# Turning the first head group's probabilities by transposing DMAs instead of TensorE in a two-layer encoder trunk

## The chip, the cores and the metric

The kernel runs on one core of a Trainium2 chip. The metric is the device time of one execution in microseconds: 1993.09 us before the change (median of three runs, 1992.59 to 1994.17). The engines of the core are named as in the profile: PE (matmul, with its weight loads as PEld), DVE (vector), ACT (scalar), POOL (gpsimd) and SP, whose queue issues nearly all DMAs.

## What is computed

Two layers of an encoder on 256 tokens of width 2048. Each layer has eight attention heads of 128 in two groups of four (each group shares one key and one value head), with a window of 128 tokens, a spatial gating part, an output projection and a gated feed-forward part with a short convolution.

```python
h = rms_norm(x, norm1_g[l])
q, k, v, gu, gv = jnp.split(h @ w_in[l], splits, axis=-1)
q = apply_rope(rms_norm(q...)); k = apply_rope(rms_norm(k...))
attn = banded_window_attention(q, k, v, sink[l])      # softmax with a sink in the denominator
sgu = chunked_spatial_gating(gelu(gu), gelu(gv), ...)  # layer norm of gv, 128x128 product, times gu
mixed = concat([rms_norm(attn), rms_norm(sgu)])
x = x + mixed @ w_o[l]
x = x + conv_gated_ffn(rms_norm(x, norm2_g[l]), w_up[l], conv_w[l], conv_b[l], w_down[l])
```

All is float32. The kernel makes a float32 product from three products of a rounded part (hi) and its rest (lo).

## The kernel before

**Weights.** They come in blocks of 1 MB. SP issues the load of a block into one of three `raw` buffers (L120), ACT rounds it in two halves to `hi` (L128, 128x1024 each, four buffers), and DVE subtracts to get `lo` (L112, four buffers). A block of the input or output projection is used by 24 matmuls of 512 columns (L168); a gate unit (L194 on) has 32 matmuls with hi (L209) and 32 half as wide with lo (L214). The blocks of a layer's input projection come as chunks of four: queries of the first group, keys and values, queries of the second group, two chunks of gv, then four gate units (gu), then w_o, w_up and w_down.

**Attention.** `attend` (L466) is a generator, made once per head group: `first` (g = 0) and `second` (g = 1). Its steps are called between weight blocks, by lists that are written out by hand (`between`, and the arguments of `gated`). The steps: take q from PSUM, rotate it and compute its norm (a power on POOL, `qr`, then L477); copy the halves of the 32-bit words apart (L422) and send them through transposing DMAs of 128x4x128 words (L429); copy them together (L435) and split them in hi and lo (L302 on ACT, L303 on DVE); then per pair of heads the products with the keys (L308 to L310, three matmuls each) into `tp`, a PSUM pool of **two** buffers, the masked scaling and maximum on DVE (L498, which empties `tp`), the exponential on ACT (L520), the sum and its inverse, and the scaling by it (L528). Then per pair of heads the probabilities are turned by PE (L536, four 128x128 transposes per 128 keys), split in parts (L302, L303, from PSUM), multiplied with the values (L308 to L310, 512 columns) and copied out of PSUM by ACT (L545).

**Gating.** gv's chunks are taken from PSUM (L723), go through a gelu on ACT (L724), statistics on DVE (L725, L729) and a power on POOL (L733, `lnr`). `normal` (L768 to L770) normalises the four `vn` tiles with tables that `gating_tables` loads (two loads at L408, six at L413); `spatial` (L751) multiplies them with the 128x128 tables, four units of 128x512 outputs.

**Order.** A scheduler orders the instructions of each engine by priority. `urgent()` raises the priority of what stands in it, weight loads and their parts among them. Every engine works through its own list in that order, and an instruction that waits holds up all behind it on its engine. `take` (L188) lets a step start only behind the matmul issued last. Tiles in SBUF come from the pool `slots` (43 of them), rows from `rowp`.

Of the kernel before, what the change touches and what calls it, by code (L numbers as in the profile page):

```python
# [8 lines left out]
F32 = mybir.dt.float32  # L9
F32R = mybir.dt.float32r  # L10
# [5 lines left out]
P = 128  # L16
# [26 lines left out]
def encoder(ctx: ExitStack, tc: tile.TileContext, xT, x, w_in, w_gu, w_o, w_up, w_down, wsT, pcol, prow, rope, out):  # L43
# [1 line left out]
    pool = lambda name, bufs, **kw: ctx.enter_context(tc.tile_pool(name=name, bufs=bufs, **kw))  # L45
    const = pool("const", 1)
    lay = pool("lay", 2)
    slots = pool("slots", 43)
    rowp = pool("rowp", 4)
    evp = pool("evp", 4)  # L50
    rawp = pool("rawp", 3)
# [8 lines left out]
        return slots.tile(shape, dt, tag="sl", name="sl")  # L60

    def row(tag):
        return rowp.tile([P, W], F32, tag=tag, name=tag)

    def ev():
        return evp.tile([P, 2, SEQ], F32, tag="ev", name="ev")
# [10 lines left out]
    def tp(shape):  # L77
        return tpp.tile(shape, F32, tag="tp", name="tp")
# [339 lines left out]
    def apart(srcs):  # L418
        halves = []
        for src in srcs:  # L420
            h = sl([P, 2, 2 * P], U16)
            nc.scalar.copy(h, src.bitcast(U16).rearrange("p (n b) -> p b n", b=2))  # L422
            halves.append(h)
        return halves

    def sent(halves):
        tall = sl([P, 4, SEQ], U16)
        for m in range(2):
            nc.sync.dma_start_transpose(tall[:, :, m * P : (m + 1) * P], halves[m].rearrange("p b n -> p (b n)"))  # L429
        return tall  # L430

    def together(tall):
# [33 lines left out]
    def attend(g, ps, r, kT, v, tab, qk, nsink, acc, pc, outs):  # L466
        ms = st([P, 2, 4], "qms")
        rot = []
        for m in range(2):
            q = row("q")  # L470
            with urgent():
                nc.scalar.activation(q, ps[:, m, :], AF.Copy, scale=r[:, m : m + 1])
            head_squares(q, 4, ms[:, m, :])
            rot.append(rotate(q, m, 4, tab))
        qr = inv_rms(ms.rearrange("p a b -> p (a b)"), HD, "q", 8)
        qs = st([P, 8], "qs")
        nc.vector.tensor_scalar_mul(qs, qr, HD**-0.5)  # L477
        rows = [rot[m].rearrange("p h d -> p (h d)") for m in range(2)]
        halves = [apart([rows[m][:, h : h + 2 * HD] for m in range(2)]) for h in (0, 2 * HD)]
        yield  # L480
        talls = [sent(h) for h in halves]
        yield
        qT = []
        for tall in talls:
            pq = parts(together(tall), [P, 2, SEQ])
            qT += [[v[:, i, :] for v in pq] for i in range(2)]
        yield
        scores = []
        for pr in range(2):
            nmx = st([P, 2, 2], "nmx")  # L490
            for i in range(2):
                h = 2 * pr + i
                t = tp([P, 2, SEQ])
                s = sl([P, 2, SEQ])
                for m in range(2):
                    matmul3(t[:, m, :], [v[:, m * P : (m + 1) * P] for v in qT[h]], [v[:, g, :] for v in kT])
                for m in range(2):
                    nc.vector.tensor_tensor_reduce(  # L498
                        out=s[:, m, :],
                        in0=t[:, m, :],  # L500
                        in1=mask[:, m, :],
                        scale=qs[:, 4 * m + h : 4 * m + h + 1],
                        scalar=LOWEST,
                        op0=ALU.add,
                        op1=ALU.max,
                        accum_out=nmx[:, i, m : m + 1],
                    )
                scores.append(s)
            h0 = 4 * g + 2 * pr
            sink = qk[:, R_SINK + h0 : R_SINK + h0 + 2].unsqueeze(2).to_broadcast([P, 2, 2])  # L510
            nsk = nsink[:, h0 : h0 + 2].unsqueeze(2).to_broadcast([P, 2, 2])
            nm = st([P, 2, 2], "nm")
            nc.vector.scalar_tensor_tensor(out=nm, in0=nmx, scalar=-1.0, in1=nsk, op0=ALU.mult, op1=ALU.min)
            es = st([P, 2, 2], "es")
            nc.vector.tensor_tensor(out=es, in0=nm, in1=sink, op=ALU.add)
            rs = st([P, 2, 2], "rs")
            for i in range(2):
                s = scores[2 * pr + i]
                for m in range(2):
                    nc.scalar.activation(s[:, m, :], s[:, m, :], AF.Exp, bias=nm[:, i, m : m + 1], accum_out=rs[:, i, m : m + 1])  # L520
            nc.scalar.activation(es, es, AF.Exp)
            nc.vector.tensor_tensor(out=rs, in0=rs, in1=es, op=ALU.add)
            rec = st([P, 2, 2], "rec")
            nc.vector.reciprocal(rec, rs)
            for i in range(2):
                s = scores[2 * pr + i]
                for m in range(2):
                    nc.vector.tensor_scalar_mul(s[:, m, :], s[:, m, :], rec[:, i, m : m + 1])  # L528
            yield
        for pr in range(2):  # L530
            pT = []
            for b in range(2):
                t = tp([P, 2, SEQ])
                for i in range(2):
                    for m in range(2):
                        nc.tensor.transpose(  # L536
                            t[:, i, m * P : (m + 1) * P], scores[2 * pr + i][:, m, b * P : (b + 1) * P], ident
                        )
                pT.append(parts(t.rearrange("p a b -> p (a b)"), [P, W]))
# [83 lines left out]
    for l in range(DEPTH):  # L623
# [48 lines left out]
        for m in range(2):  # L672
# [2 lines left out]
                out=a, in0=a, in1=rk[:, 2 * m : 2 * m + 2].unsqueeze(2).to_broadcast([P, 2, HD]), op=ALU.mult  # L675
            )
            krot.append(a)
        vs = [parts(kv[m][:, 2 * HD :], [P, 2 * HD]) for m in range(2)]
        kT = []

        khalves = apart([a.rearrange("p h d -> p (h d)") for a in krot])
# [24 lines left out]
        r1b = as_rows(r1)  # L706
        second = group_steps(1, ps)
        second()
        ws, lrows = gating_tables(l)


        vn = []
        stats = st([P, 2, 2, 6], "bns")
        for i in range(2):
            if l:
                between = [[[first], [first], [], [first]], [[first, second], [first], [second, first], [second]]]
            else:
                between = [[[first], [first], [first], [second]], [[second], [], [first], [first]]]
            ps = chunk(3 + i, between[i])
            for m in range(2):  # L720
                t = row("vn")
                with urgent():
                    nc.scalar.activation(t, ps[:, m, :], AF.Copy, scale=r1[:, m : m + 1])  # L723
# [218 lines left out]
```

## Time and profile before

| | |
|---|---|
| the three runs | 1992.59, 1993.09, 1994.17 us |
| the profiled execution | 1992.69 us, of which its span is 1990.9 us |
| PE clock granted | 1.000 |
| DMA | 391.15 MB, 196 GB/s on average |
| weight load of 1 MB, issue to landing | 4.9 to 5.2 us |

The profile is of one execution of the kernel. Its page gives busy times by engine, the span in 40 slices, DMA queues, the chain of work that ended last and the costliest groups of instructions; further views list waits, groups by line and shape, and instructions in order of time. A row of the view in order of time holds the start, the time to the end of the row's last instruction, engine and line, and after x how many instructions were merged in it. The stage that the change touches lies between 70 and 180 us (layer 0) and between 1063 and 1180 us (layer 1).

### The profile page before, as it was taken

The numbers are of one execution on the slowest core, as the hardware profiler recorded it, in microseconds if no ns is written. First come the engines' busy times: TensorE is split into PE (matmuls) and PEld (weight loads), VectorE is DVE, ScalarE is ACT, GpSimd is POOL, SyncE is SP. The second block draws the span as 40 slices with busy tenths as digits, with TensorE's granted clock in tenths as the row PEclk, the third lists the DMA queues.
The fourth block names the chain that finished last, engine by engine and source line by source line (L and its number), as shares of the span: only waits on it lengthen the run. The fifth ranks groups of instructions, "written<-read, shape, count | busy, mean of one in ns | idle before, by whom it ended". The sixth has DMA issues, their size and how long they took to land.

```text
span 1990.9 us, 26332 instructions
## 1 busy us (share of the span) xinstructions
PE 1985.5 (100%) x10292; PEld 1704.8 (86%) x10292; DVE 1367.6 (69%) x1930; ACT 1134.5 (57%) x1514; POOL 23.3 (1%) x25
## 2 busy tenths in 40 slices
PE   9999999999999999999999999999999999999999
PEld 8888888888888888888888888888888888888887
DVE  6778677777754577775566786777777445777753
ACT  6786585556543455556667675855555344555542
POOL 0100000000000000000000000000000000000000
PEclk9999999999999999999999999999999999999999
DMA  9754674455555544556767536745545554455563
GB/s 341 243 161 149 219 222 169 170 208 207 198 191 192 188 170 174 212 207 204 219 205 237 161 142 226 198 169 206 207 180 211 191 192 167 171 208 203 201 212 127
DMA packets 95580, 391.15 MB, mean 196 GB/s; under 512 B 43744, under 2 KB 45024, under 8 KB 50912
## 3 DMA queue, kind: packets, MB, share of 16 engines
q1 hardware_dynamic: 94736, 388.74, 56.6%
q8 instruction: 80, 1.31, 0.3%
q10 hardware_dynamic: 720, 0.73, 0.1%
q14 instruction: 44, 0.36, 0.1%
HBM read 378.43 MB, written 2.10 MB: 191 GB/s over the span
## 4 chain that ended last, share of the span: by engine, by line
PE 97%; ACT 1%; DVE 1%; DMA 1%; issue 0%; SPq 0%; POOL 0%; DVEq 0%; ACTq 0%
PE mm L168 42%; PE mm L234 31%; PE mm L240 16%; PE mm L209 2%; PE mm L275 1%; PE tp L168 1%; PE mm L214 1%; PE mm L270 1%; PE tp L308 0%; PE tp L751 0%; PE tp L310 0%; DVE lo L112 0%; PE tp L309 0%; DMA raw<-in_w_up 0%; ACT hi L128 0%
## 5 line engine op out<-in xcount | busy, mean ns | idle before, releaser
L112 DVE TENSOR_TENSOR lo<-raw,hi 128x1024 fp32r<-128x1024 f32 (+1 forms) x708 | 839.4, 1215 | 417.4 <-ACT hi L128 277.1
L128 ACT ACTIVATE hi<-raw 128x1024 fp32r<-128x1024 f32 (+1 forms) x708 | 730.3, 1050 | 606.8 <-PE mm L168 330.9
L168 PE MATMUL mm<-hi,sl 128*128 128x512 f32 x2480 | 667.6, 390 | 0.1
L234 PE MATMUL mm<-sl,hi 128*128 128x512 f32 x2688 | 617.8, 389 | 0.2 <-ACT hi L128 0.2
L234 PEld LDWEIGHTS mm<-sl,hi 128*128 128x128 f32 x2688 | 501.9, 188 | 103.5 <-ACT hi L128 1.1
L168 PEld LDWEIGHTS mm<-hi,sl 128*128 128x128 f32 x2480 | 464.5, 188 | 97.2 <-DVE sl L289 0.9
L168 PE MATMUL mm<-lo,sl 128*128 128x512 f32 x1240 | 382.6, 390 | 0.0
L240 PEld LDWEIGHTS mm<-sl,lo 128*128 128x128 f32 x2688 | 328.1, 192 | 3.3
L240 PE MATMUL mm<-sl,lo 128*128 128x256 f32 x2688 | 329.1, 283 | 0.0
L168 PEld LDWEIGHTS mm<-lo,sl 128*128 128x128 f32 x1240 | 232.5, 188 | 47.9
L838 DVE SCALAR_TENSOR_TENSOR sc<-ev,pc,sc 128x255 f32<-128x255 f32 x176 | 80.6, 481 | 94.0 <-ACT sc L837 94.0
L281 ACT COPY ev<-mm 128x512 f32<-128x512 f32 x96 | 55.4, 577 | 122.5 <-PE mm L240 114.8
L837 ACT ACTIVATE sc<-ev,pc 128x256 f32<-128x256 f32 x176 | 99.1, 589 | 0.0
L841 DVE SCALAR_TENSOR_TENSOR sc<-ev,pc,sc 128x255 f32<-128x255 f32 x176 | 80.6, 481 | 2.9
L296 ACT ACTIVATE sl<-sl 128x256 fp32r<-128x256 f32 x88 | 31.8, 409 | 72.8 <-DVE sl L857 72.8
L283 DVE TENSOR_TENSOR ev<-mm,ev 128x512 f32<-128x512 f32 x96 | 65.6, 683 | 0.0
L209 PE MATMUL mm<-sl,hi 128*128 128x512 f32 x256 | 61.6, 391 | 0.0
L833 DVE TENSOR_TENSOR ev<-ev,rb 128x512 f32<-128x512 f32 x88 | 60.1, 682 | 0.1
L209 PEld LDWEIGHTS mm<-sl,hi 128*128 128x128 f32 x256 | 47.3, 188 | 9.2
L289 DVE SCALAR_TENSOR_TENSOR sl<-sl,pc 128x256 fp32r<-128x256 f32 x96 | 42.6, 479 | 17.7 <-ACT sl L288 17.6
L297 DVE TENSOR_TENSOR sl<-sl 128x256 fp32r<-128x256 f32 x88 | 33.5, 422 | 19.4 <-ACT sl L296 19.4
L288 ACT ACTIVATE sl<-sl,pc 128x256 fp32r<-128x256 f32 x96 | 43.2, 497 | 1.1 <-DMA sl<-in_xT 0.9
(124 smaller groups left out, 813.2 us busy)
## 6 DMA issues: line engine op xcount, KB each, us to landing
raw<-in_w_up SPq DMA_DIRECT2D x172, 1024.0 KB, 5.2
raw<-in_w_down SPq DMA_DIRECT2D x88, 1024.0 KB, 4.9
raw<-in_w_in SPq DMA_DIRECT2D x38, 1024.0 KB, 5.1
raw<-in_w_o SPq DMA_DIRECT2D x32, 1024.0 KB, 4.9
raw<-in_w_gu SPq DMA_DIRECT2D x16, 1024.0 KB, 4.9
raw<-in_w_up SPq DMA_DIRECT2D x8, 512.0 KB, 4.5
sl<-in_prow SPq DMA_DIRECT2D x12, 256.0 KB, 7.3
raw<-in_w_in SPq DMA_DIRECT2D x8, 256.0 KB, 5.2
```

What stands on the lines that cost most here:

```text
L112: nc.vector.tensor_tensor(out=lo, in0=part, in1=hi.bitcast(F32), op=ALU.subtract)
L128: nc.scalar.activation(hi[:, cs], part, AF.Copy)
L168: nc.tensor.matmul(ps[m], acts[kk][:, part % 2, m * P : (m + 1) * P], w, start=first and kk == 0 and part == 0, stop=last and kk == KB - 1 ...
L209: nc.tensor.matmul(ps[:, i, :], tile_of(his, k, i), x1, start=k == 0, stop=False)
L234: nc.tensor.matmul(pss[n][:, i, :], hs[k // KB][:, c : c + P], x1, start=k == 0, stop=False)
L240: nc.tensor.matmul(pss[n][:, i, :SEQ], los[k // KB][:, c : c + P], acts[k][:, 0, :], start=False, stop=k == len(acts) - 1)
L281: nc.scalar.copy(rest, ps[:, :, SEQ:])
L283: nc.vector.tensor_tensor(out=s, in0=ps[:, :, :SEQ], in1=rest, op=ALU.add)
L833: nc.vector.tensor_tensor(out=s, in0=s, in1=r2b2[0], op=ALU.mult)
L837: nc.scalar.activation(t[:, i, :], s[:, i, :], AF.Identity, bias=col(3), scale=col(1))
L838: nc.vector.scalar_tensor_tensor(out=t[:, i, 1:], in0=s[:, i, : SEQ - 1], scalar=col(0), in1=t[:, i, 1:], op0=ALU.mult, op1=ALU.add)
L841: nc.vector.scalar_tensor_tensor(out=t[:, i, : SEQ - 1], in0=s[:, i, 1:], scalar=col(2), in1=t[:, i, : SEQ - 1], op0=ALU.mult, op1=ALU.add)
```

## The change

For the first group the sixteen PE transposes of a layer go. Behind the scaling of a pair's scores, ACT copies each head's tile apart into two halves of 16-bit words (L538), SP sends each through one DMA transpose of 128x8x128 words (L547), and DVE joins the halves again in the layout that PE wrote before (L559, two copies for each 128 keys of a pair); the parts hi and lo then come from SBUF. The second group keeps the transposes on PE (now L565). The first group has two more steps, and the hand-written lists are shared out anew. The transposes of keys and queries become urgent (L430). The gating tables are asked for behind the two gv chunks instead of ahead of them. Values' hi and lo share a slot, q's four copies of 128x512 become two of 128x1024 (L483), `slots` grows from 43 to 46 and the rows for q shrink from four to two.

```diff
-    slots = pool("slots", 43)
+    slots = pool("slots", 46)
...
-        return rowp.tile([P, W], F32, tag=tag, name=tag)
+        return rowp.tile([P, W], F32, tag=tag, name=tag, bufs=2 if tag == "q" else 4)
...
     def sent(halves):
         tall = sl([P, 4, SEQ], U16)
-        for m in range(2):
-            nc.sync.dma_start_transpose(tall[:, :, m * P : (m + 1) * P], halves[m].rearrange("p b n -> p (b n)"))
+        with urgent():
+            for m in range(2):
+                nc.sync.dma_start_transpose(tall[:, :, m * P : (m + 1) * P], halves[m].rearrange("p b n -> p (b n)"))
...
-        halves = [apart([rows[m][:, h : h + 2 * HD] for m in range(2)]) for h in (0, 2 * HD)]
+        both = []
+        for m in range(2):
+            t = sl([P, 2, 2, 2 * HD], U16)
+            words = rot[m].rearrange("p h d -> p (h d)").bitcast(U16)
+            nc.scalar.copy(t, words.rearrange("p (j n b) -> p j b n", j=2, b=2))
+            both.append(t)
+        halves = [[t[:, pr, :, :] for t in both] for pr in range(2)]
...
+                if g == 0:
+                    with urgent():
+                        h = sl([P, 2, 2, SEQ], U16)
+                        nc.scalar.copy(h, s.bitcast(U16).rearrange("p m (k b) -> p m b k", b=2))
+                    flat.append(h)
+            yield
+
+        tall = []
+        for pr in range(2 if g == 0 else 0):
+            for i in range(2):
+                with urgent():
+                    t = sl([P, 2, 2, 2, P], U16)
+                    nc.sync.dma_start_transpose(
+                        t.rearrange("p m b c n -> p (m b c) n"), flat[2 * pr + i].rearrange("p m b k -> p (m b k)")
+                    )
+                tall.append(t)
             yield
...
+                if g == 0:
+                    t = sl([P, W])
+                    words = t.bitcast(U16).rearrange("p (i m n b) -> p i b m n", i=2, m=2, b=2)
+                    for i in range(2):
+                        nc.vector.tensor_copy(words[:, i], tall[2 * pr + i][:, :, :, c, :].rearrange("p m b n -> p b m n"))
+                else:
+                    t = tp([P, W])
...
-        vs = [parts(kv[m][:, 2 * HD :], [P, 2 * HD]) for m in range(2)]
+        vs = []
+        for m in range(2):
+            t = sl([P, 2, 2 * HD], F32R)
...
-        ws, lrows = gating_tables(l)
...
-                between = [[[first], [first], [], [first]], [[first, second], [first], [second, first], [second]]]
+                between = [[[first], [first], [], [first]], [[first, second], [first], [second, first], [first, second]]]
             else:
-                between = [[[first], [first], [first], [second]], [[second], [], [first], [first]]]
+                between = [[[first], [first], [first], [second]], [[second, first], [first], [first], [first]]]
...
+        ws, lrows = gating_tables(l)
...
-            gated(0, [second], [])
+            gated(0, [first, second], [])
```

The order moves with this at three places that matter below, all in layer 1.

SP's list around the first gate loads (`raw<-in_w_gu`), before with -, of the change with +; L429 and L430 are the second group's query transposes, L547 the first group's probabilities:

```order
 L120 DMA raw<-in_w_gu 128x2048 x3
-L429 DMA_TRANSPOSE sl<-sl 128x4x128
-L120 DMA raw<-in_w_gu 128x2048
-L429 DMA_TRANSPOSE sl<-sl 128x4x128 x3
-L120 DMA raw<-in_w_gu 128x2048 x3
-L120 DMA raw<-in_w_o 128x2048 x14
-L582 DMA_TRANSPOSE sl<-sl 128x4x128 x2
-L120 DMA raw<-in_w_o 128x2048
+L547 DMA_TRANSPOSE sl<-sl 128x8x128 x4
+L430 DMA_TRANSPOSE sl<-sl 128x4x128 x4
+L120 DMA raw<-in_w_gu 128x2048 x5
```

Eight transposes now stand together ahead of the fourth gate load, where one small one stood behind it.

DVE's list around the third block of the first gv chunk, before; `qs_9285` is the second group's query scale, which comes from POOL, the rest are weight parts:

```order
L323 TENSOR_SCALAR qv_9281<-qms_9258 128x8
L453 TENSOR_TENSOR sl_9275<-sl_9275,sl_9277 128x512
L477 TENSOR_SCALAR qs_9285<-qr_9283 128x8
L112 TENSOR_TENSOR lo_9502<-raw_9495,hi_9501 128x1024
L112 TENSOR_TENSOR lo_9559<-raw_9556,hi_9558 128x1024
```

The same place in the change's list; `tp_9324` is the PSUM buffer with the first group's first scores, and PE's next scores of that group (`tp_9400`) take its place:

```order
L323 TENSOR_SCALAR qv_9273<-qms_9250 128x8
L454 TENSOR_TENSOR sl_9267<-sl_9267,sl_9269 128x512
L478 TENSOR_SCALAR qs_9277<-qr_9275 128x8
L504 ISA sl_9325,nmx_9323<-tp_9324,mask_130,qs_9079 128x256
L504 ISA nmx_9323 128x1
L112 TENSOR_TENSOR lo_9482<-raw_9475,hi_9481 128x1024
L504 ISA sl_9325,nmx_9323<-tp_9324,mask_130,qs_9079 128x256
L504 ISA nmx_9323 128x1
```

The reading of the scores now stands in that place, with a weight part between its two halves; PE asks for `tp_9400` 13 matmuls into this third block, where before no scores were asked for until the following chunk.

ACT's list at gate unit 0, in the change; `raw_9959` is the fourth gate load, `tp_9660` holds the first group's first product with the values, and `sl_9650` is an operand of the second group's scores:

```order
L302 ACTIVATE sl_9610<-sl_9607 128x512
L758 ACTIVATE vn_9766<-vn_9766 128x512
L128 ACTIVATE hi_9955<-raw_9949 128x1024
L436 COPY sl_9648<-sl_9560 128x2x512
L302 ACTIVATE sl_9650<-sl_9648 128x512
L128 ACTIVATE hi_9961<-raw_9959 128x1024
L436 COPY sl_9654<-sl_9563 128x2x512
L302 ACTIVATE sl_9656<-sl_9654 128x512
L128 ACTIVATE hi_9965<-raw_9959 128x1024
L574 COPY sl_9667<-tp_9660 128x512
```

The copy that empties `tp_9660` stands behind both weight parts of the fourth gate load; before, that product was taken one chunk earlier and its copy (L545) stood ahead of the gate units.

More of the change, by code (lines that the diff above doesn't have):

```diff
@@ L477, in attend @@
         nc.vector.tensor_scalar_mul(qs, qr, HD**-0.5)
-        rows = [rot[m].rearrange("p h d -> p (h d)") for m in range(2)]
-        halves = [apart([rows[m][:, h : h + 2 * HD] for m in range(2)]) for h in (0, 2 * HD)]
+        both = []
[5 more added lines that the diff above has]
+        halves = [[t[:, pr, :, :] for t in both] for pr in range(2)]
         yield
@@ L487, in attend @@
         yield
-        scores = []
+        scores, flat = [], []
         for pr in range(2):
@@ L531, in attend @@
             pT = []
[L532 to L539, printed above, removed]
+            for c in range(2):
+                if g == 0:
[5 more added lines that the diff above has]
+                    t = tp([P, W])
+                    for i in range(2):
+                        for m in range(2):
+                            at = (2 * i + m) * P
+                            nc.tensor.transpose(
+                                t[:, at : at + P], scores[2 * pr + i][:, m, c * P : (c + 1) * P], ident
+                            )
+                pT.append(parts(t, [P, W]))
             yield
@@ L677, in encoder @@
             krot.append(a)
-        vs = [parts(kv[m][:, 2 * HD :], [P, 2 * HD]) for m in range(2)]
+        vs = []
+        for m in range(2):
+            t = sl([P, 2, 2 * HD], F32R)
+            v = kv[m][:, 2 * HD :]
+            nc.scalar.activation(t[:, 0, :], v, AF.Copy)
+            nc.vector.tensor_tensor(out=t[:, 1, :], in0=v, in1=t[:, 0, :].bitcast(F32), op=ALU.subtract)
+            vs.append([t[:, 0, :], t[:, 1, :]])
         kT = []
```

## The prediction

> **What bounds the kernel now.** I read the page first: busy times, the clock in 40 slices, the chain that ended last.
>
> ```profile
> span 1990.9 us, 26332 instructions
> PE 1985.5 (100%) x10292; PEld 1704.8 (86%) x10292; DVE 1367.6 (69%) x1930; ACT 1134.5 (57%) x1514; POOL 23.3 (1%) x25
> PEclk9999999999999999999999999999999999999999
> PE 97%; ACT 1%; DVE 1%; DMA 1%; issue 0%; SPq 0%; POOL 0%; DVEq 0%; ACTq 0%
> ```
>
> TensorE works through the whole span at a full clock, and the chain runs over it. The view of waits says the same of PE:
>
> ```profile
> PE tp L99 <- DVE ones L95: 1.1, 1, 1.1
> PE mm L234 <- ACT hi L128: 0.2, 1, 0.2
> PE tp L308 <- DVE sl L303: 0.2, 1, 0.2
> ```
>
> So whatever leaves PE shortens the kernel by its issue pitch, and whatever PE newly waits for lengthens it in full. Other engines count only there. Matmuls overlap, so their starts are compared, not their durations:
>
> ```profile
> L536 PE MATMUL tp<-ident,sl 128*128 128x128 f32 x64 | 9.7, 280 | 0.0
> 1102.97 1.12 PE L536 MATMUL tp<-ident,sl 128*128 128x128 f32 x8
> 1103.84 0.94 PE L168 MATMUL mm<-hi,sl 128*128 128x512 f32 x3
> 1110.21 0.48 PE L168 MATMUL mm<-hi,sl 128*128 128x512 f32 x1
> 1110.70 0.66 PE L536 MATMUL tp<-ident,sl 128*128 128x128 f32 x4
> 119.68 6.74 PE L209 MATMUL mm<-sl,hi 128*128 128x512 f32 x29
> 126.61 0.47 PE L308 MATMUL tp<-sl 128*128 128x512 f32 x1 [0.20 <-DVE sl L303]
> ```
>
> **The gain.** Of the 64 transposes, the first group's 32 go (16 in each layer). Eight of them take 1103.84 - 1102.97 = 0.87 us, 109 ns each: 32 x 109 ns = **3.5 us**. By the group row (9.7 us over 64, 152 ns with what surrounds them) it would be 4.9 us; I take 3.5, since a start follows a start. Some short pauses beside them go too. A 512-wide matmul has a pitch of 0.23 us (29 of them, 119.68 to 126.35); the L308 at 126.61 is 0.3 us late and the L536 at 1110.70 0.26 us late. With smaller ones at the other places I put these at **1.0 us**, an estimate (0.5 to 1.4).
>
> [...]
>
> **What is added.** Per layer ACT copies four score tiles apart (128x1024 words), SP issues four DMA transposes twice as large as any before, DVE joins with eight copies of 128x512 words, and the gating tables (8 loads) are asked for later.
>
> ```profile
> 1099.35 5.87 SPq L120 DMA_DIRECT2D raw<-in_w_gu  x2
> 1107.98 1.20 SPq L429 DMA_TRANSPOSE sl<-sl  x1
> 108.80 5.24 SPq L429 DMA_TRANSPOSE sl<-sl  x4
> 87.06 0.90 SPq L408 DMA_DIRECT2D sl<-in_wsT  x2
> raw<-in_w_gu SPq DMA_DIRECT2D x16, 1024.0 KB, 4.9
> sl<-sl SPq DMA_TRANSPOSE x68, 4.5
> sl<-in_prow SPq DMA_DIRECT2D x12, 256.0 KB, 7.3
> L435 ACT COPY sl<-sl 128x1024 uint16<-128x1024 uint16 x10 | 13.5, 1352 | 0.7 <-DMA sl<-sl 0.7
> L302 ACT ACTIVATE sl<-sl 128x512 fp32r<-128x512 f32 x10 | 6.3, 633 | 0.3
> L303 DVE TENSOR_TENSOR sl<-sl 128x512 fp32r<-128x512 f32 x10 | 6.9, 689 | 5.7 <-ACT sl L302 5.7
> L768 DVE TENSOR_SCALAR vn<-vn,mv,lnr 128x512 f32<-128x512 f32 x8 | 4.3, 543 | 0.8 <-POOL lnr L733 0.8
> L528 DVE TENSOR_SCALAR sl<-sl,rec 128x256 f32<-128x256 f32 x32 | 9.1, 348 | 0.2
> L498 DVE CUSTOM_DVE_ANT_0 sl<-tp,mask,qs 128x256 f32<-128x256 f32 x32 | 14.0, 478 | 0.2 <-PE tp L310 0.2
> L733 POOL TENSOR_TENSOR lnr<-lnv,mhalf 128x2 f32<-128x2 f32 x2 | 1.4, 697 | 106.3 <-DVE lnv L731 106.3
> ```
>
> An apart-copy is 1.35 us, 5.4 us per layer. The joining copy is shown nowhere: 0.35 to 0.7 us (L528 to L303), I take 0.5, so 4 us per layer. ACT and DVE have that time idle; it costs only where PE's operand stands behind it. A 128 KB transpose holds SP for 1.25 us (and lands after 4.5), a plain load for 0.45. The 256 KB transpose is unknown: 1.25 us if the size doesn't matter, 2.5 if it goes by bytes; with the 0.45 as a fixed part and 0.8 for each four blocks it is **2.05 us**, the value I take. The tables land about 7.3 us after their issue; DVE first uses them behind a unit's last lo, by my walk some 10 us after it, and the spatial products (L786) come over 20 us after it, so moving them costs nothing while that gap lasts. What is hidden on DVE beside this, joining copies included, costs at most a few tenths. Sharing buffers and the one larger q copy remove two ACT instructions per group and add no wait that I can place.
>
> [...]
>
> **The new waits of PE**, walked on the trace's clock with the new order.
>
> ```profile
> 84.82 0.69 DVE L453 TENSOR_TENSOR sl<-sl 128x512 f32<-128x512 f32 x1
> 86.59 1.06 ACT L128 ACTIVATE hi<-raw 128x1024 fp32r<-128x1024 f32 x1
> 87.91 0.62 PE L168 MATMUL mm<-lo,sl 128*128 128x512 f32 x2
> 115.24 6.87 SPq L120 DMA_DIRECT2D raw<-in_w_gu  x2
> 120.39 1.24 ACT L723 ACTIVATE vn<-mm,xr 128x512 f32<-128x512 f32 x2
> 1076.55 1.07 PE L168 MATMUL mm<-hi,sl 128*128 128x512 f32 x4
> 1077.18 0.17 DVE L477 TENSOR_SCALAR qs<-qr 128x8 f32<-128x8 f32 x1 [1.53 <-POOL qr L325]
> 1077.27 2.36 DVE L112 TENSOR_TENSOR lo<-raw,hi 128x1024 fp32r<-128x1024 f32 x2
> 1111.89 7.44 PE L209 MATMUL mm<-sl,hi 128*128 128x512 f32 x32
> ```
>
> W1, layer 0, the first group's query-key products move one chunk forward, behind 23 matmuls of a block (PE there at 87.91 + 0.23 = 88.1). ACT has ahead of their operand: the second q copy from 85.5 (the L453 at 84.82 ends), 1.35; hi, 1.06; L436, 1.35; L302, 0.63: done at 89.7 to 89.9. The wait is up to 1.7 us; 0 if ACT does the weight part first. I take **1.2**.
>
> W2, layer 0, first products with the probabilities. DVE's L303 that PE needs stands behind L803, which waits for POOL's power. From the L757 pair (120.39 + 1.24 = 121.6): gelu 0.6, hi 1.05, gelu 0.6, bn_stats 0.7, aggregate and add 0.4, POOL 0.7, L803 0.54, L303 0.69: about 127. PE, 24 matmuls and four more behind 119.68, is there at 126.1, and the second pair repeats 0.7. The walk says 1.6, before shows a pause of 0.3 to 0.4 at this place; I take **1.2** (0.4 to 2.5, the upper end if the transposes behind the load issued at 115.24 land late).
>
> W3, layer 1, second half of the first group's query-key products, moved into the third block of the first gv chunk. They need one of two PSUM buffers, which DVE frees with two L504. These stand behind L478, which waits for POOL until 1077.18, and a lo of 1.2 us stands between the two: 1077.35 + 0.48 + 1.2 + 0.48 = 1079.5. PE is there 13 matmuls into the block, at 1076.55 + 0.23 = 1076.8. **2.7** (1.5 to 3).
>
> W4, layer 1, gate unit 0 (from 1111.89 in before). SP now issues four large and four small transposes between the loads that came at 1099.35 and 1104.89: 4 x 2.05 + 4 x 1.25 = 13 us, the next load about 8 us later than now. ACT's weight part of that load stands ahead of L574, which frees a PSUM buffer for the second group's products. Load 4.9, hi 1.06, L436 1.35, L302 0.63, hi 1.06, L574 0.58: some 3 us behind PE by the large estimate of 2.05, none at 1.25, 4 to 5 at 2.5. In the same unit PE waits for L303 behind L803, as in W2. Taken together **2.4** (0.5 to 4.5).
>
> **The sum**, against the profiled execution's own 1992.69 us (its span of 1990.9 and 1.8 around it): -3.5 - 1.0 + 1.2 + 1.2 + 2.7 + 2.4 = +3.0, that is **1995.7 us**. The median of the runs is 0.4 above that execution, less than their spread; I leave it out.
>
> **Rivals.** A measurement of this kernel tells about 0.2% (4 us) from no change, so the borders are 1989.1 and 1997.1.
>
> R1, the waits are covered. For it: before is built of the same waits and shows pauses of 0.4 us at most; PE's lead or the weight buffers may give way. Against it: W3's chain is in rows as it stands. -3.5 - 1.0 with 0 to 1 of waits: 1988.2 to 1989.2.
>
> R2, the other side: the large transposes block the weight queue. One place, SP in layer 1 ahead of the delayed load. It decides from 2.5 us on SP per transpose; at 3 us, the delay grows by 4 x 0.95 = 3.8, W4 becomes about 6.5 and the time 1992.69 - 4.5 + 5.1 + 6.5 = 1999.8. For it: size alone already takes SP from 0.45 to 1.25. Against it: a part of that must be fixed.
>
> R3, the large transpose takes SP no longer than the small one (1.25). W4 falls to about 0.5, and the time is 1993.8. [...]
>
> **How the numbers follow.** Forecast 0.45 (same 0.32, slower 0.13), R1 0.23 (faster 0.18, same 0.05), R2 0.20 (slower), R3 0.12 (same): faster 0.18, same 0.49, slower 0.33. The range runs from R1's low end to the sum with W1 to W4 at 1.7, 2.5, 3.0 and 4.5 less half a microsecond, as all four won't be at their ends: 1988.2 to 1999.5, widened to 2000.5 for R2.
>
> **What would show it.** In the new profile: 32 rows of transposes left on PE; pauses at the first L308 behind 13 matmuls in layer 1 (2 to 3 us, DVE L478 waiting for POOL ahead of it); SP's row for the 128x8x128 transposes near 2 us each; the load behind them at 13 us distance instead of 5.5; L574 late in layer 1. It would be wrong if PE shows no pause over 0.5 us in both layers' attention stages (then R1), or if PE waits for the gating tables, which I cost at nothing.

## The result and the profile after

The changed kernel takes **2005.61 us** (median of four runs, 2003.06 to 2007.93) against 1992.84 us before on the same chip (1991.27 to 1994.17): ratio 1.0066, 95% interval 1.0054 to 1.0078. It is slower by 12.8 us; the forecast was +3.0, and the range ended at 2000.5.

The profiled execution took 2004.51 us. Its page, the totals:

```profile
span 2002.7 us, 26283 instructions
PE 1987.3 (99%) x10260; PEld 1704.8 (85%) x10260; DVE 1372.3 (69%) x1946; ACT 1141.2 (57%) x1513; POOL 21.5 (1%) x25
```

The span is 11.8 us longer than before, though PE has 32 instructions less. Its waits (source line, engine and line waited for; total, times, longest, in us):

```profile
PE tp L308 <- ACT sl L302: 3.0, 2, 1.8
PE tp L308 <- DVE nmx L504: 2.3, 1, 2.3
PE tp L308 <- ACT sl L574: 2.1, 1, 2.1
PE mm L168 <- DVE lo L112: 1.6, 2, 1.1
PE tp L309 <- DVE sl L303: 1.1, 1, 1.1
```

Before, this list held 0.4 us in the two layers. Each of the four predicted waits is here: W1 and half of W2 in the first row, W3 in the second, W4 in the third, the other half of W2 in the fifth. The operations that were added or changed, from the groups by line and shape (busy us, mean ns of one, then the engine's idle time before them):

```profile
L565 PE MATMUL tp<-ident,sl 128*128 128x128 f32 x32 | 5.1, 275 | 0.0
L538 ACT COPY sl<-sl 128x1024 uint16<-128x1024 uint16 x8 | 8.0, 1035 | 0.0
L559 DVE COPY sl<-sl 128x512 uint16<-128x512 uint16 x16 | 6.8, 452 | 1.8 <-DMA sl<-sl 1.8
```

The change did what it says: 32 transposes are left on PE. The copies cost less than was taken (1.04 us instead of 1.35, 0.45 instead of 0.5), and neither is long enough to matter by itself.

**Where the 11.8 us are.** A pause is taken here as the distance between two matmuls beyond the pitch (0.227 us for 512 columns, 0.120 for 256, by 64 matmuls of L234 in 14.53 us and 64 of L240 in 7.67 before the change; 0.109 for a transpose); all those over 0.04 us behind the first 5.6 us of the kernel add up to 8.0 us before and 22.8 us after. That is 14.8 us more, less 32 x 0.109 = 3.5: 11.3 us. The other 0.5 us is spread over distances below that bound.

| term | predicted | measured |
|---|---|---|
| transposes gone | -3.5 | -3.5 |
| older small pauses gone | -1.0 | -3.4 |
| W1, start of the scores, layer 0 | 1.2 | 2.4 |
| W2, first products with values, layer 0 | 1.2 | 1.4 + 1.7 |
| W3, second half of the scores, layer 1 | 2.7 | 2.6 |
| W4, gate unit 0, layer 1 | 2.4 | 3.2 |
| half clock behind W2 and behind W4 | no term | 2.5 + 1.5 |
| w_o, layer 0 (two pauses) and layer 1 (one) | no term | 1.5 + 1.4 |

A piece of 4.0 us is in no wait at all. Busy time in three stretches around W2 (length; busy us and instructions of PE, PEld, DVE, ACT, POOL; granted clock; DMA share; GB/s):

```profile
126.00:130.00 4.00, 1.82 (x7) 0.86 (x5) 2.52 (x7) 1.58 (x2) 0.70 (x1) 0.94 1.00 223
130.00:134.00 4.00, 3.91 (x10) 3.13 (x11) 2.68 (x7) 0.72 (x2) 0.00 (x0) 0.50 0.95 342
134.00:138.00 4.00, 4.00 (x25) 3.81 (x25) 0.88 (x2) 2.98 (x5) 0.00 (x0) 0.71 0.49 188
```

PE stands still for 3.1 us in two pauses, and from 129.49 to 136.32 us the granted clock is 0.50: PE is shown nearly fully busy, with 10 matmuls in the second stretch, at distances of 0.427 us where 0.227 is its pitch. The pauses ahead of it are short: W2 is two pauses of 1.4 and 1.7 us with four matmuls between them, and W4 is one of 2.3 us, with a clock of 0.53 from 1132.80 to 1136.20 us. What the traces show of the clock behind short pauses is in the last section.

### The profile page after: what moved, and what is told of

It reads as the page before. It is cut to its first block, busy times and chain, and to the rows that moved or that the text cites. A ratio compares the mean times of both kernels' runs of the same rounds, so it can differ in the third digit from the quotient of the medians.

```text
span 2002.7 us, 26283 instructions
## 1 busy us (share of the span) xinstructions
PE 1987.3 (99%) x10260; PEld 1704.8 (85%) x10260; DVE 1372.3 (69%) x1946; ACT 1141.2 (57%) x1513; POOL 21.5 (1%) x25
## 4 chain that ended last, share of the span: by engine, by line
PE 96%; DVE 1%; ACT 1%; DMA 1%; issue 0%; POOL 0%; SPq 0%; DVEq 0%; ACTq 0%; POOLq 0%
PE mm L168 40%; PE mm L234 30%; PE mm L240 16%; PE mm L209 2%; PE mm L275 1%; PE mm L214 1%; PE tp L168 1%; PE mm L270 1%; DVE lo L112 1%; DMA sl<-sl 1%; PE tp L308 0%; PE tp L309 0%; PE tp L786 0%; PE tp L310 0%; ACT hi L128 0%
## 5 line engine op out<-in xcount | busy, mean ns | idle before, releaser
L112 DVE TENSOR_TENSOR lo<-raw,hi 128x1024 fp32r<-128x1024 f32 (+1 forms) x708 | 839.1, 1214 | 421.6 <-ACT hi L128 269.5
L128 ACT ACTIVATE hi<-raw 128x1024 fp32r<-128x1024 f32 (+1 forms) x708 | 730.7, 1051 | 601.3 <-PE mm L168 323.1
L234 PE MATMUL mm<-sl,hi 128*128 128x512 f32 x2688 | 617.2, 389 | 0.0
L234 PEld LDWEIGHTS mm<-sl,hi 128*128 128x128 f32 x2688 | 502.1, 188 | 102.5
L240 PEld LDWEIGHTS mm<-sl,lo 128*128 128x128 f32 x2688 | 328.1, 192 | 3.3
L240 PE MATMUL mm<-sl,lo 128*128 128x256 f32 x2688 | 329.1, 283 | 0.0
L288 ACT ACTIVATE sl<-sl,pc 128x256 fp32r<-128x256 f32 x96 | 43.1, 496 | 1.1 <-DMA pc<-in_pcol 0.5
```

The costliest lines, as they stand in the source:

```text
L112: nc.vector.tensor_tensor(out=lo, in0=part, in1=hi.bitcast(F32), op=ALU.subtract)
L128: nc.scalar.activation(hi[:, cs], part, AF.Copy)
L234: nc.tensor.matmul(pss[n][:, i, :], hs[k // KB][:, c : c + P], x1, start=k == 0, stop=False)
L240: nc.tensor.matmul(pss[n][:, i, :SEQ], los[k // KB][:, c : c + P], acts[k][:, 0, :], start=False, stop=k == len(acts) - 1)
```

## The experiments

Each is timed beside the kernel before on the same chip, whose median was 1992.5 to 1993.3 us throughout; the ratio is to that. An edit is of the changed kernel unless something else is said.

### The tables alone

Two questions come first: does the loss come from turning by DMA, or from the order in which the rest now stands? The kernel before, with only the tables moved:

```diff
-        ws, lrows = gating_tables(l)
...
+        ws, lrows = gating_tables(l)      # behind the two gv chunks
```

> The kernel before, with the gating tables asked for behind the gv chunks and nothing else; all probabilities still turned on TensorE. Theory A (the order makes the loss, and the moved tables make the order of the query-key products): the second half of layer 1's first query-key products stands 13 matmuls into the third block of a gv chunk, as in the changed kernel, and TensorE pauses there 2 to 3 us; the kernel is 1 to 4 us slower than before, 1994 to 1997 us. Theory B (the transposing DMAs and their joining make the loss): within 1 us of before, no pause over 0.5 us.

Measured: 1995.86 us, 1.0015 (1.0006 to 1.0024). PE in order of time in layer 0 and in layer 1 (start, time, engine, line, operation, operands, count; in brackets the idle time before it and its releaser):

```profile
89.81 0.39 PE L308 MATMUL tp<-sl 128*128 128x256 f32 x1 [1.36 <-ACT sl L302]
...
1081.16 0.38 PE L308 MATMUL tp<-sl 128*128 128x256 f32 x1 [2.70 <-DVE nmx L498]
```

W1 and W3 stand here, behind the same instructions, without a single DMA transpose of probabilities. With the tables' requests moved, the scheduler puts the query-key products earlier on PE, where their operands (layer 0) and their PSUM buffer (layer 1) aren't ready. That it does so because the tables no longer take buffers ahead of the attention would explain it; no run shows it. "Moving them costs nothing" counted the loads, and not what moves up into their place.

### The tables back, everything else changed

The opposite edit, in the changed kernel:

```diff
+        ws, lrows = gating_tables(l)      # ahead of the gv chunks again
...
-        ws, lrows = gating_tables(l)
```

> The changed kernel with the gating tables asked for where they were before, all else as changed. Theory A: the pauses of about 2.1 us (layer 0) and 2.6 us (layer 1) ahead of the first group's query-key products go, 4 to 5 us less than the changed kernel, about 2001 us, if the probabilities' own waits stay. Theory B: no change against the changed kernel's 2005.6 us, within 2 us.

Measured: 2015.74 us, 1.0114 (1.0099 to 1.0129). W1 and W3 go as expected (0.5 and 0 us left), but the time was missed by far: new pauses come later, the longest at the start of w_o in layer 0 (PE in order of time):

```profile
185.28 0.77 PE L308 MATMUL tp<-sl 128*128 128x512 f32 x1 [7.48 <-DVE nmx L504]
```

Behind it 512-wide matmuls stand 0.43 us apart, half clock again. So the old place isn't free any more with the longer chain and its buffers. That `slots` runs short would explain it; no run shows it.

### The changed order without DMA turning

```diff
-                if g == 0:          # L535, apart; the same at L555, joined
+                if False:
...
-            for i in range(2):      # L544, the DMA transposes
+            for i in range(0):
```

> The changed kernel with the first group's probabilities turned on TensorE again (no large transposes, no apart-copies of scores, no joining copies); lists, tables and buffers as changed. Theory A: the two pauses ahead of the query-key products stay (2.1 and 2.6 us), the later ones at gate unit 0 of both layers fall under 0.5 us each, and no stretch runs at half clock; with 3.5 us of transposes back the time is 1995 to 1999 us. Theory B: back to 1993 us.

Measured: 1997.78 us, 1.0021 (1.0011 to 1.0031). Waits of PE:

```profile
PE tp L308 <- ACT sl L302: 3.6, 1, 3.6
PE tp L308 <- DVE nmx L504: 2.2, 1, 2.2
```

W1 and W3 stay, W2 and W4 go (nothing over 0.3 us in the gate units). The time is as expected, but half clock is not gone: the wait at W1 is 3.6 us here, and a stretch of 3.4 us at half clock follows it. This splits the 12.8 us: some 4.5 us belong to lists, tables and buffers, some 8 us to turning by DMA in this order, with its 3.5 us of saving already taken off.

### Four edits, one for each cause

**W2 and W4, the work ahead of the needed instruction on DVE and ACT.** The joining copies, the splitting and the copy L574 are made urgent:

```diff
+                    with urgent():           # L556, joined copies, and parts() behind them
...
+            with urgent():                   # L574
```

> The changed kernel with the joining copies, the split of the joined probabilities in hi and lo, and the copy of the product out of PSUM marked urgent. Theory A: in gate unit 0 the split no longer stands behind the normalising of vn that waits for POOL, the pauses there shrink from 3.1 us (layer 0) and 3.2 us (layer 1) to under 1 us each, the half-clock stretches behind them (about 4 us of matmul time in all) go, and the time is 1996 to 2000 us. Theory B: the landing of the large transposes sets these waits, and the time stays over 2003 us.

Measured: 2005.69 us, 1.0067 (1.0050 to 1.0083): no change. W4 stays at 2.5, W2 at 1.5 and 1.4. The joining copies start when the transposes land, at 125.11 and 126.60 us, as without the edit. For the split and for L577 (L574 before) the run says less, since the order there did not move. DVE in layer 0, in order of time; L806 is the line that was L803:

```profile
128.89 0.55 DVE L806 TENSOR_SCALAR vn<-vn,mv,lnr 128x512 f32<-128x512 f32 x1 [0.81 <-POOL lnr L771]
129.35 0.69 DVE L303 TENSOR_TENSOR sl<-sl 128x512 fp32r<-128x512 f32 x1
```

In layer 1 ACT still has both weight parts (1125.94 and 1128.82 us) ahead of L577 at 1129.76. What another order would do at these two places is not shown by this run.

**W4, the load held behind the small transposes.**

```diff
-        with urgent():
-            for m in range(2):
-                nc.sync.dma_start_transpose(...)   # L430, keys and queries
+        for m in range(2):
+            nc.sync.dma_start_transpose(...)
```

> The changed kernel with the key and query transposes (L430) no longer urgent, so that in layer 1 the fourth gate load stands on SP directly behind the four large transposes and ahead of the second group's four small ones. Theory A (ACT's weight part of the late load holds the copy that frees PSUM): the load is issued about 5 us earlier, TensorE's pause of 2.3 us in gate unit 0 of layer 1 falls under 0.7 us and the half clock behind it goes; 2001 to 2003.5 us against 2005.6. Rival C (the second group's operands are late by themselves): the pause stays within 0.5 us of 2.3, or comes back at the next products; over 2004 us.

Measured: 2000.36 us, 1.0039 (1.0025 to 1.0053), 5 us better. SP in order of time (an x4 row holds four issues), first of the changed kernel, then of this one, whose lines stand one lower:

```profile
1098.39 11.56 SPq L120 DMA_DIRECT2D raw<-in_w_gu  x3
1110.01 7.68 SPq L547 DMA_TRANSPOSE sl<-sl  x4
1117.72 5.21 SPq L430 DMA_TRANSPOSE sl<-sl  x4
1123.03 1.00 SPq L120 DMA_DIRECT2D raw<-in_w_gu  x2
```

```profile
1107.99 7.68 SPq L546 DMA_TRANSPOSE sl<-sl  x4
1115.78 0.52 SPq L120 DMA_DIRECT2D raw<-in_w_gu  x1
```

Counted from the first large transpose, the fourth gate load goes 5.2 us sooner, and the 2.3 us pause behind L574 is gone. One of 1.15 us is left at the first product with the values. Not all of the 5 us are due to the load: in the profiled execution W2's half clock of 2.5 us is gone too, though W2's pauses are as long as they were, and 1.4 us of half clock stand behind W3 instead.

**W3, the products that moved up in layer 1.** The first group's step behind the second block moves behind the third:

```diff
-                between = [[[first], [first], [], [first]], ...
+                between = [[[first], [], [first], [first]], ...
```

> The changed kernel with one step of the list in layer 1 moved by one weight block, so that the second half of the first group's query-key products comes behind the third block and not behind the second. Theory A: the pause of 2.6 us ahead of these products goes (under 0.5 us), and the time falls by 2 to 3 us, to about 2003 us. Rival C (the work is late anyway, and a pause taken away at one place comes back at the next): the pauses in gate unit 0 grow by as much, and the time stays over 2004.5 us.

Measured: 2000.93 us, 1.0043 (1.0028 to 1.0058), 4.7 us better, more than the 2 to 3 expected. W3 is gone, W4 stays at 2.5. The profiled execution also has 0.9 us less of half clock, behind W1 and W2 instead of W2 and W4.

**W2, transposes held behind loads in layer 0.** The steps are drawn forward, so that they are asked for earlier:

```diff
-                between = [[[first], [first], [first], [second]], [[second, first], [first], [first], [first]]]
+                between = [[[first], [first], [first], [first, second]], [[second, first], [first], [first], []]]
```

> The changed kernel with one step of the list in layer 0 moved by one block, so that the first two large transposes stand on SP ahead of the two gate loads that wait for a weight buffer, not behind them. Theory A2 (the landing of the large transposes, held up on SP behind these loads, makes layer 0's pauses of 1.4 and 1.7 us): the joining copies start before 120 us instead of 125.1, both pauses together fall from 3.1 to under 1 us, no half clock at 130 us, time 2000.5 to 2003 us. Rival D (the power on POOL and the normalising ahead of the split make them, as the prediction had it): the second pause stays over 1 us.

Measured: 2002.50 us, 1.0053 (1.0038 to 1.0068), 3.1 us better, though by its interval, which overlaps that of the changed kernel, the times alone don't show a gain. What was expected is there in part: the second pause of W2 falls to under 0.3 and the clock stays full behind the place, but the first is 2.2 us, and W1 in this execution is 3.9. The joining copies start at 126.70 us, not before 120. They no longer wait for a landing: they stand on DVE behind weight parts, one of which waited 3.87 us for ACT. Some 12 us ahead of W1 a copy L436 on ACT waited 2.58 us for a small transpose to land; whether that made W1 longer was not traced.

### The edits together, and DMA turning in one layer

Layer 0 as before the change (its tables, its list, TensorE turning), layer 1 with DMA turning and the edits against W3 and W4:

```diff
-                if g == 0:
+                if g == 0 and dma[0]:        # dma[0] is the layer, at all three places
...
+        if not l:
+            ws, lrows = gating_tables(l)     # layer 0, ahead of the gv chunks
```

> Layer 0 as before the change (transposes on TensorE, tables early, its old list), layer 1 as changed with both edits of the runs before (the scores' step one block later, query transposes not urgent). Theory A: without the waits the gain is the 16 transposes of one layer, 1.75 us, less what pauses remain in gate unit 0 (0 to 1.5 us): 1991.5 to 1994 us beside 1993.3. Rival C: pauses of over 2 us remain in layer 1, 1995 us or more.

Measured: 1992.97 us, 1.0000 (0.9991 to 1.0010), as by theory A. All three edits (L430, and both lists), with both layers turned by DMA:

> The three edits of e5, e6 and e7 together (query transposes not urgent; the scores' step one block later in layer 1; the first two large transposes one block earlier in layer 0), both layers through the DMAs. If the pauses are additive, 2005.6 less 5.2, 4.7 and 3.1: about 1993 us. If each edit alone also took away half-clock stretches that the others share, less is left to gain: 1995 to 1998 us, with pauses of 2 to 4 us ahead of layer 0's query-key products and about 2 us at its gate unit 0 still there.

Measured: 1993.19 us, 1.0002 (0.9993 to 1.0012). The edits add up: 1.0066 less 0.0027, 0.0023 and 0.0013 is 1.0003. So two lists and one priority make up for the whole loss, with every DMA transpose in its place. Yet nothing is gained either, and the next runs ask why.

### Two attempts at a gain

Beside the edits on W3 and W4, the scores of layer 0 two blocks later:

```diff
-                between = [[[first], [first], [first], [second]], [[second, first], [first], [first], [first]]]
+                between = [[[first], [], [], [first, second]], [[first], [first], [second, first], [first]]]
...
-            gated(1, [second, first], [])
+            gated(1, [second, first], [first])
```

> The edits of e5 and e6, and in layer 0 the first group's scores two blocks later and everything behind them later too, so that its products with the values come in the third gate unit. Theory A (what PE waits for is late by its place in the lists, not by the DMAs' own time): no pause over 1 us ahead of layer 0's query-key products nor at its first products with the values, and no half clock; 1993 to 1996 us. Rival C: the pauses come back between the gate units and w_o in layer 0 (over 3 us there), 1997 us or more.

Measured: 2002.37 us, 1.0049 (1.0032 to 1.0066). W1 and W2 go, but layer 0 gets new pauses of 1.3 us in its gate units and 1.0, 1.5, 1.1, 1.0 and 3.6 us in w_o, with half clock behind them, as by rival C. And layer 1 alone, with the joining and L574 made urgent as above:

> As e8 (layer 1 alone), with the joining copies, their split and the copy out of PSUM urgent, in search of a version faster than both. If the pause of 1.2 us at layer 1's gate unit 0 goes and the two at the start of w_o (1.2 and 0.8 us) stay: 1991.5 to 1992.5 us. If all stay: 1993 us as e8.

Measured: 1998.08 us, 1.0027 (1.0017 to 1.0037), worse by 5 us than without it, where 1991.5 to 1993 was expected: new pauses of 1.2 us in the gate units of layer 1 and 2.1 us at its w_o. Both failed in one way: a step that is put elsewhere to end one wait is late, or in the way, at the next place.

### The three edits, with TensorE turning

Is turning by DMA worth its 3.5 us where the order is mended? The three edits again, with the edit `if False` of above.

> The three edits of list and order together (1993.2 us with the DMA turning), but with the first group's probabilities turned by TensorE again: no L538, L547 and L559, 64 transposes of 109 ns instead of 32. Theory: the 3.5 us of transposes are a real saving and the loss of the change lies in the order alone. Then this kernel has 3.5 us more of transposes, keeps the pause at the start of the scores in layer 0 (2.0 us, which ends behind copies of ACT that have nothing to do with the turning), and loses the pauses of 0.8 (layer 0) and 1.15 us (layer 1) that end behind landed probabilities or the load held behind them: 1993.2 + 3.5 - 0.8 to -2 = 1994.7 to 1995.9 us. Rival: the turning by DMA costs what it saves wherever it stands (ACT's copies apart, transposes in front of loads), so this one is at 1992.7 us or below, faster than the same order with the DMA turning. Either way by the sum of pauses over 40 ns in the trace and by the rows of transposes on TensorE: 64 of them.

Measured: 1992.07 us, 0.9998 (0.9989 to 1.0007). My theory missed, and the time is the rival's: giving the 3.5 us back to PE costs nothing. Transposes and waits of PE with DMA turning, and then with TensorE turning:

```profile
L564 PE MATMUL tp<-ident,sl 128*128 128x128 f32 x32 | 4.7, 276 | 0.0
...
PE tp L308 <- ACT sl L302: 3.2, 3, 1.7
PE mm L168 <- ACT sl L288: 0.9, 1, 0.9
```

```profile
L564 PE MATMUL tp<-ident,sl 128*128 128x128 f32 x64 | 8.6, 274 | 0.1
...
PE tp L308 <- ACT sl L302: 1.7, 1, 1.7
```

All pauses together, counted as above, are 11.8 us with DMA turning and 7.5 with TensorE: 4.3 us come back for the 3.5 that are saved. Most of it is at the first products with the values in layer 0 (0.84 against 0.16 us) and in layer 1 (1.15 against 0.17), and at the start of w_o in layer 1 (1.15 and 0.81 against nothing over 0.1), which the theory left out. ACT in order of time at the second of them, with DMA turning:

```profile
1115.10 1.06 ACT L128 ACTIVATE hi<-raw 128x1024 fp32r<-128x1024 f32 x1 [1.30 <-DMA raw<-in_w_gu]
1116.58 0.63 ACT L302 ACTIVATE sl<-sl 128x512 fp32r<-128x512 f32 x1 [0.41 <-DVE sl L558]
```

ACT waits for a load that was issued behind the transposes, and then for the joining copy. The pause at w_o ends behind ACT's L288; why that is late only with DMA turning was not traced. By times alone the two kernels can't be told apart, since their intervals overlap; by the trace, turning by DMA is no gain even here.

## Why the prediction was wrong

The places of the four waits were right; the step that failed is their price in the sum. A pause was priced by its length alone, with no term for the half clock behind it (4.0 us measured). W2 was laid to POOL, and not to large transposes that SP issues late (3.1 us for 1.2). W1 was discounted below its walk (2.4 for 1.2). And w_o (2.9 us) had no term.

**The bound and the gain** were right: what left PE counted by its pitch, 32 x 109 ns, and what PE waited for counted in full: the two give 11.3 of the 11.8 us.

**W1** was the right place and chain, undersized: 2.4 us for 1.2. ACT, then PE, in order of time:

```profile
86.30 1.05 ACT L483 COPY sl<-sl 128x1024 uint16<-128x1024 uint16 x1 [0.35 <-DVE sl L454]
...
88.22 1.32 ACT L436 COPY sl<-sl 128x1024 uint16<-128x1024 uint16 x1
89.57 0.63 ACT L302 ACTIVATE sl<-sl 128x512 fp32r<-128x512 f32 x1
```

```profile
88.03 0.39 PE L168 MATMUL mm<-lo,sl 128*128 128x512 f32 x1
90.25 0.39 PE L308 MATMUL tp<-sl 128*128 128x256 f32 x1 [1.83 <-ACT sl L302]
```

The walk had the second copy from 85.5 us; it started at 86.30, since DVE's rotation ended later. PE came at 88.26, close to the 88.1 predicted. And of a walk that said up to 1.7 I took 1.2, a discount for which no row spoke.

**W2** was the term with the wrong cause. The forecast let DVE's L303 wait for POOL, and took 1.2; the 2.5 "if the transposes behind the load issued at 115.24 land late" was kept as an end of the range. It was that case. SP, then DVE, then PE in order of time:

```profile
114.30 4.49 SPq L120 DMA_DIRECT2D raw<-in_w_gu  x2
118.84 7.80 SPq L547 DMA_TRANSPOSE sl<-sl  x4
```

```profile
125.11 0.47 DVE L559 COPY sl<-sl 128x512 uint16<-128x512 uint16 x1 [0.88 <-DMA sl<-sl]
...
126.60 0.45 DVE L559 COPY sl<-sl 128x512 uint16<-128x512 uint16 x1 [0.94 <-DMA sl<-sl]
...
128.89 0.55 DVE L803 TENSOR_SCALAR vn<-vn,mv,lnr 128x512 f32<-128x512 f32 x1 [0.81 <-POOL lnr L768]
129.35 0.68 DVE L303 TENSOR_TENSOR sl<-sl 128x512 fp32r<-128x512 f32 x1
```

```profile
127.77 0.50 PE L308 MATMUL tp<-sl 128*128 128x512 f32 x1 [1.14 <-ACT sl L302]
...
130.09 0.79 PE L309 MATMUL tp<-sl 128*128 128x512 f32 x1 [1.13 <-DVE sl L303]
```

ACT had taken the last scores apart at 110.9 us (its L538 row starts at 108.94 and takes 1.98), but SP came to the transposes only at 118.84, behind two loads, and its second issue took 3.79 us by itself (below). DVE, in order, waited for the landing twice; so the statistics at 126.95, POOL's power and L803 came late as well, and L303 behind them. In this trace the landing made both pauses, the second by the predicted chain. The run with earlier requests agrees for the second pause, which is gone there. Its first is still 2.2 us with the probabilities long landed, so an early landing alone does not end W2: DVE's order then holds it.

**W3** was right in place, chain and size, 2.6 us for 2.7. DVE, then PE, in order of time:

```profile
1084.49 0.17 DVE L478 TENSOR_SCALAR qs<-qr 128x8 f32<-128x8 f32 x1 [1.53 <-POOL qr L325]
...
1084.97 1.22 DVE L112 TENSOR_TENSOR lo<-raw,hi 128x1024 fp32r<-128x1024 f32 x1
```

```profile
1086.65 0.39 PE L308 MATMUL tp<-sl 128*128 128x256 f32 x1 [2.31 <-DVE nmx L504]
```

Its origin was not seen: the tables.

**W4** was right in its chain and about right in size: three small pauses (0.9 us together) and one of 2.3. The load went 13.4 us behind the one ahead of it (1109.63 to 1123.03), as forecast, and nearly at the forecast's price: the four large transposes held SP for 7.68 us, 1.92 us each in the mean, the four small ones for 5.21. But the mean hides that they are not alike. SP in order of time, the second of the four in each layer:

```profile
120.12 3.79 SPq L547 DMA_TRANSPOSE sl<-sl  x1
1111.29 3.66 SPq L547 DMA_TRANSPOSE sl<-sl  x1
```

The other six take 1.23 to 1.34 us. ACT's copies apart don't explain it: in layer 0 they had ended at 110.9 us, and in layer 1 at 1113.2, where this issue ends at 1114.95. Before the change, by SP's list above, one small transpose stood ahead of the fourth gate load and three behind it; the sentence under that list has it otherwise. ACT in order of time, then PE:

```profile
1128.30 1.06 ACT L128 ACTIVATE hi<-raw 128x1024 fp32r<-128x1024 f32 x1 [2.29 <-DMA raw<-in_w_gu]
...
1131.18 1.04 ACT L128 ACTIVATE hi<-raw 128x1024 fp32r<-128x1024 f32 x1
1132.12 0.56 ACT L574 COPY sl<-tp 128x512 f32<-128x512 f32 x1
```

```profile
1132.74 0.38 PE L308 MATMUL tp<-sl 128*128 128x256 f32 x1 [2.05 <-ACT sl L574]
1133.99 2.33 PE L214 MATMUL mm<-sl,lo 128*128 128x256 f32 x10
```

**What the sum lacked** are the 4.0 us of half clock behind W2 and W4, seen in the last row: ten half-wide matmuls in 2.33 us, 0.21 apart instead of 0.12. They are the largest single part of the miss. Then come 2.9 us at w_o, W2 (1.9 us), W1 (1.2) and W4 (0.8); 2.4 us more of small old pauses gone than forecast stand against them. The pauses at w_o end behind weight parts (L128 on ACT, L112 on DVE); why these are late was not traced.

**The rivals.** R1 (the waits are covered) fell. R2 had the right side and the right queue, but its 3 us per transpose is above the mean of 1.9, and its "size alone" is not in the rows: before the change plain loads of 1 MB held SP for 0.33 us (L120 at 90.52), transposes of 128 KB for 1.20 to 1.34 (L429); its place in layer 1 cost what the forecast had. R3's 1.25 us fits six of the eight issues, but the second of each four takes three times that. "Wrong if PE waits for the gating tables" was the wrong question: PE never does.

## What to carry over

A request that is moved costs what moves into its place, and that is read from the new order of all engines, not from the duration of what was moved. In the changed kernel the half clock behind W2 and W4, with 2.1 and 2.3 us of stand-still ahead of it within 3.41 us, cost 2.5 and 1.5 us beyond the pauses themselves; for such pauses a sum needs a chance of that loss. The estimate of a wait is not to be discounted below its own walk. A large DMA transpose held SP for 1.23 to 1.34 us, the second of four for 3.66 and 3.79; it landed 3.1 to 6.5 us after its issue and has copies of 1.04 and 0.45 us around it. Where these didn't all fit ahead of the products, PE waited: with the three edits, of the 3.5 us saved, some 0.7 us came back as waits in layer 0 and some 3 us in layer 1.

## What was not expected of the hardware

- **The clock after short pauses.** It fell behind W2's 1.4 + 1.7 us and behind W4's 2.3 us, but not behind W3's 2.6 us in the same execution. In the run with L430 not urgent, W3 lasted 2.05 us and the granted clock was 0.70 in the four us behind it, where after W3's 2.6 us it was 1.00. In the changed kernel's execution two stretches ran at 0.50, of 6.83 us from 129.49 and of 3.41 us from 1133.01: the starts are 1003.52 us apart, 294 times 3.413. In each of the 14 traces every half-clock stretch between the kernel's first and last 10 us lasted 3.41 us or twice that, and their starts lay whole multiples of 3.41 us apart, on a grid that lay elsewhere in each execution. Cut each of the 14 traces along its own grid, and add up how long PE stands still (distances over 0.04 us beyond the pitch) in each window that runs at full clock: of the 18 windows with 2.00 us or more, 17 were followed by half clock, and of those with less, at most 1.97 us, none was. One window of the run with earlier requests, with 2.05 us, is the exception. What sets the clock was not shown. Two windows of the changed kernel at W3, then two at W4 (columns as above):

```profile
1081.81:1085.22 3.41, 2.54 (x12) 1.76 (x10) 1.88 (x8) 2.50 (x4) 2.00 (x1) 1.00 0.06 24
1085.22:1088.63 3.41, 1.98 (x14) 1.90 (x15) 3.39 (x9) 1.08 (x1) 0.00 (x0) 1.00 0.44 96
1129.60:1133.01 3.41, 1.36 (x12) 1.15 (x11) 1.06 (x2) 3.35 (x5) 0.00 (x0) 1.00 0.09 34
1133.01:1136.42 3.41, 3.41 (x18) 3.41 (x18) 1.76 (x2) 1.14 (x3) 0.00 (x0) 0.50 0.00 0
```

A border at 1085.22 cuts W3 in two, 1.0 and 1.6 us, and the clock stayed at 1.00; 2.3 us of stand-still fall into one window at W4, and 0.50 followed. W2's first pause and the start of its second share the window that ends at 129.49, 2.1 us in all. If these windows set the price of a pause, it is luck where a pause falls on the grid, and with it part of what each edit above gained or lost; no run tests it. That an equal pause has a different price fits the wider spread of the changed kernel's runs (4.9 us for four runs, before 2.9).
- **The second of the large transposes issued in a row held SP for 3.79 us in layer 0 and 3.66 in layer 1.** The changed kernel's other six took 1.23 to 1.34 us. The ten runs with large transposes all show it: 3.6 to 4.1 us, once 5.3 (with the three edits, layer 0). In the run with earlier requests layer 0 issues them in two pairs, and the second of each pair is the long one (3.85 and 3.67 us). Why was not found.
- **The landing went with the place in the row.** In both layers of the changed kernel the first two of the four large transposes landed 5.8 to 6.5 us after their issue, the last two 3.1 to 4.0 us.
